# A two-layer hybrid decoder on one core: first projections from a transposed x, its root applied afterwards

## The chip, the cores and the metric

The kernel runs on one core of a Trainium2 chip. The metric is device time in microseconds, from timed runs of the whole program. Beside these there is one profiled execution, from which all views come. The engines are called PE (TensorE, with its weight loads as PEld), DVE (VectorE), ACT (ScalarE), POOL (GpSimd) and SP (SyncE, which issues nearly all DMAs).

## The reference

Two layers, x of 512 tokens by 1024 channels, all in float32. Per layer:

```
h = RMSNorm_pre(x)                       # x * rsqrt(mean(x*x) + 1e-6) * g_pre, per token
q_h, f_h, i_h, z_h, q_a, k_a, v_a, z_a = split(h @ W_in)
o_h = hgrn2(q_h, f_h, i_h) -> per-head RMSNorm, * silu(z_h)
q_a, k_a = rotary(q_a), rotary(k_a)      # 16 query heads, 2 key/value heads of 64
o_a = sliding-window attention (128) with sinks, * silu(z_a)
x = x + RMSNorm_post(concat(o_h, o_a) @ W_out)
```

The root of a token, rsqrt(mean(x*x) + 1e-6), is one number per token. So h @ W equals (x * g_pre) @ W with each token's row multiplied by its root afterwards.

## The kernel before

**Arithmetic.** Every large product is done as three matmuls in a rounded float type: each operand is split into a high part (a cast on ACT) and a low part (value minus high part, on DVE or POOL), and high·high, high·low and low·high are added in PSUM. The activations stand transposed, as `hT[l] = (hhi, hlo)`, 128 channels per partition block (8 blocks k) by 512 tokens.

**Weights.** All weights are one long list of pieces of 128 by 512 (256 KB), planned at L115 to L140 in the order of use: four of keys/values (`("kv", 0)`), then eight per slab of 512 columns, first the two query slabs `QA` and `QA + 1`. `w_load` (L156) issues a piece's DMA on SP into one of four raw buffers; `w_conv` (L165) makes high part (L181, ACT) and low part (L182, DVE, or POOL for pieces in `on_pool` with an odd number) in one of nine buffers each. A piece's load waits until the piece four before it is converted.

**Order.** `pin` (L84) keeps an instruction in the order in which the program issues it on its engine; other instructions may be moved by the scheduler that arranges the program when it is built. A `Unit` (L217) is one output tile: eight steps k of three matmuls each. `step` (L276) does one unit step, and two units run alternately from the half of the first on. `later(n, key, fn)` (L202) runs a function n steps on. `plan_conversions` (L247) gives each piece a step by which its conversion is issued. `merge` (L50) mixes steps with attention and recurrence work.

**The head of layer 0.** x comes in rows, four tiles `xts` of 128 tokens (L990 to L1005), with the kv pieces between them on SP. Per tile a `Norm` (L368) does: squares with a sum on ACT (L383, L386), the root on POOL (L354 or L391 and L393), scaling by root and gain on DVE (L401), eight transposes on PE (L406), high part on ACT (L410), low part on DVE (L414). The gain is spread over the partitions by eight transposes into two PSUM tiles (L1020). L1024 to L1074 write the order out by hand: tile 0 first, then kv for tile 0, with the later tiles' `half` calls between the kv steps. `kv_evac` (L448) copies a kv tile out of PSUM and loads the rotary tables; `kv_rotate` (L460) and `kv_store` (L486) rotate and transpose the keys.

**Queries.** `qa_stream` (L501) runs the four units of a query slab, m = 0 to 3, one after another (two at a time overlapping). `evac` multiplies the result by the cosine and sine tables on DVE (L510 to L517); at odd m POOL combines them (L520, L521), and `rest` splits (L526, L527), writes a stack to DRAM (L529) and reads it back in another layout (`load_q`, L497). Attention begins `QWAIT` steps after the second stack (L977 to L980). `constants` (L1089) loads masks and small parameters and prepares them, 36 steps after the start.

Of the kernel before, what the change touches and what calls it, by code (L numbers as in the profile page):

```python
# [25 lines left out]
EPS = 1e-6  # L26
# [6 lines left out]

W_BUFS = 9
# [36 lines left out]
def hybrid_kernel(ctx: ExitStack, tc: tile.TileContext, x, wkv, win, wout, g_pre, g_post, lbp, ghead, sinks,  # L71
# [50 lines left out]
    def plan_in(l, s):  # L122
        plan(("in", l, s), [win[l, s, k * P:(k + 1) * P, :] for k in range(KT)])
# [23 lines left out]
    in_turn = set(range(KT // 2, KT))  # L147
# [6 lines left out]
    state = {"raw": 0, "conv": 0, "limit": KT // 2}  # L154
# [92 lines left out]
    def plan_conversions():  # L247
# [15 lines left out]
        for p in reversed(range(len(pieces))):  # L263
            late = min(late, first[p] - LEAD) if p not in kv_pieces else late
            due.insert(0, late)
            late -= SPACE
# [101 lines left out]
    class Norm:  # L368
# [12 lines left out]
        def square(self, c=None, whole=None):  # L381
            if c is None:
                return pin(nc.scalar.activation(self.hT[1][:, :, self.tt * P:(self.tt + 1) * P],  # L383
                                                whole.rearrange("p a (k t) -> p (a k) t", t=P), AF.Square,
                                                scale=1.0 / 32.0, accum_out=self.ss[:, 0:1]))
            return nc.scalar.activation(self.hT[1][self.part(c)], self.xt[c].rearrange("p (k t) -> p k t", t=P), AF.Square,  # L386
                                        scale=1.0 / 32.0, accum_out=self.ss[:, c:c + 1])

        def power(self):
            t = sm.tile([P, 1], F32, tag="s1", name="s1")  # L390
            pin(nc.gpsimd.tensor_scalar(t, self.ss[:, 0:1], EPS, None, op0=ALU.add))  # L391
            self.r = sm.tile([P, 1], F32, tag="r1", name="r1")
            pin(nc.gpsimd.tensor_tensor(self.r, t, mhalf[:, 0:1], op=ALU.pow))  # L393

        def square_halves(self):
            for c in range(2):
                pin(self.square(c))
            self.r = rstd2(self.ss, pin)
# [44 lines left out]
    def layer(l, last):  # L443
# [3 lines left out]

        def kv_evac(tt, o):  # L448
            if tt == 0:
                rkv.append(big.tile([P, NT, 256], F32, tag="oy", name="rkv", bufs=6))  # L450
                rot.append(big.tile([P, 2, 512], F32, tag="q", name="cs", bufs=QB))
                nc.sync.dma_start(rot[0][:, 0], cos_f)
                nc.sync.dma_start(rot[0][:, 1], sin_f)
            nc.scalar.copy(rkv[0][:, tt], o)
            if tt == NT - 1:
                later(12 if l == 0 else 8, None, kv_rotate)
                later(24 if l == 0 else 16, ("k", l, 0), kv_store)


        def kv_rotate():  # L460
# [8 lines left out]
            kk = rkv_rot()  # L469
# [505 lines left out]
        def run():  # L975
            rest = lambda key: (through(key), remaining(key))
            until(lambda: 1 in qs)  # L977
            for _ in range(QWAIT):
                step()
# [200 lines left out]
```

## Time and profile before

| | us |
|---|---|
| timed runs, median (lowest to highest) | 921.15 (920.98 to 921.52) |
| profiled execution, its own time | 922.98 |
| its span | 921.3 |
| busy: PE, PEld, DVE, ACT, POOL | 904.2, 752.5, 667.0, 463.8, 273.9 |
| first kv matmul, first query matmul start | 10.06, 26.92 |

In the views, a timeline row gives start, duration, engine, line, operation, output<-inputs, shape and count, and in brackets how long the engine had been idle and what ended that. A group row ends in busy time, mean ns of one, idle time before it. Durations of matmuls overlap, so their pace is read from the distance of the starts.

### The profile page before, as it was taken

To read this page: it belongs to the slowest core of one execution; us is meant where nothing else is said; L and a number is where in the kernel's file an instruction comes from. 1 tells how busy PE (TensorE), PEld (TensorE's weight loads), DVE (VectorE), ACT (ScalarE), POOL (GpSimd) and SP (SyncE) were. 2 spreads that over 40 slices of the span, in tenths; PEclk is the share of its full clock that TensorE was granted. 3 is DMA by queue.
4 is the path that set the end of the run, shared out by engine and by line. 5 is a ranking of instruction groups with operands and counts; after the bars stand their busy time and mean duration, and the time that the engine had idled before them with its cause. 6 is when DMAs were issued, how large, how long until landed. Compare 5 with 4: busy or idle time off the path is not lost.

```text
span 921.3 us, 19004 instructions
## 1 busy us (share of the span) xinstructions
PE 904.2 (98%) x7240; PEld 752.5 (82%) x7240; DVE 667.0 (72%) x1326; ACT 463.8 (50%) x1100; POOL 273.9 (30%) x292
## 2 busy tenths in 40 slices
PE   8999999999999999999999999999999999999996
PEld 6888887888888888888888878888888888888885
DVE  4977878859854797655786689776889449866556
ACT  5535757653664423534563466686446463245242
POOL 3424444303413042121332254451144022330102
PEclk9999999999999999999999999999999999999999
DMA  7594613322222332333355656122322323213413
GB/s 224 153 259 130 172 43 92 92 81 85 91 69 70 107 103 82 92 95 119 131 168 167 168 141 179 57 70 92 94 70 81 99 73 94 82 47 93 137 35 137
DMA packets 56570, 100.74 MB, mean 109 GB/s; under 512 B 6560, under 2 KB 9120, under 8 KB 56480
## 3 DMA queue, kind: packets, MB, share of 16 engines
q1 hardware_dynamic: 56192, 99.40, 36.4%
q8 instruction: 57, 0.93, 0.4%
q14 instruction: 33, 0.27, 0.1%
q10 hardware_dynamic: 288, 0.14, 0.1%
HBM read 86.93 MB, written 12.58 MB: 108 GB/s over the span
## 4 chain that ended last, share of the span: by engine, by line
PE 89%; DVE 6%; ACT 2%; issue 1%; POOL 1%; DMA 0%; POOLq 0%; DVEq 0%; ACTq 0%
PE pj L293 73%; PE sc L567 2%; PE ac L620 2%; PE sc L750 2%; PE ac L821 2%; DVE wlo L182 1%; PE ac L824 1%; PE ac L808 1%; PE sc L594 1%; ACT s L581 1%; PE sc L873 1%; PE sc L406 1%; PE sc L796 1%; DVE a L954 0%; PE sc L556 0%
## 5 line engine op out<-in xcount | busy, mean ns | idle before, releaser
L182 DVE TENSOR_TENSOR wlo<-raw,whi 128x512 fp32r<-128x512 f32 x249 | 182.8, 748 | 49.5 <-ACT whi L181 48.8
L181 ACT CAST whi<-raw 128x512 fp32r<-128x512 f32 x256 | 154.1, 620 | 105.9 <-PE pj L293 95.1
L293 PE MATMUL pj<-hhi,wlo 128*128 128x512 f32 x512 | 203.8, 398 | 0.0
L293 PE MATMUL pj<-hhi,whi 128*128 128x512 f32 x512 | 199.8, 390 | 0.0
L293 PE MATMUL pj<-hlo,whi 128*128 128x512 f32 x512 | 199.5, 390 | 0.0
L293 PE MATMUL pj<-whi,ops 128*128 128x512 f32 (+1 forms) x520 | 172.5, 394 | 0.0
L293 PEld LDWEIGHTS pj<-whi,ops 128*128 128x128 f32 x520 | 97.3, 188 | 19.3
L293 PEld LDWEIGHTS pj<-hhi,whi 128*128 128x128 f32 x512 | 96.1, 188 | 20.7
L293 PEld LDWEIGHTS pj<-hhi,wlo 128*128 128x128 f32 x512 | 96.2, 188 | 19.3
L293 PEld LDWEIGHTS pj<-hlo,whi 128*128 128x128 f32 x512 | 96.2, 188 | 18.6
L293 PE MATMUL pj<-whi,hlo 128*128 128x512 f32 x256 | 103.6, 405 | 0.0
L293 PE MATMUL pj<-wlo,ops 128*128 128x512 f32 (+1 forms) x260 | 100.8, 388 | 0.0
L293 PE MATMUL pj<-wlo,hhi 128*128 128x512 f32 x256 | 100.4, 392 | 0.3 <-DVE wlo L182 0.2
L293 PE MATMUL pj<-whi,hhi 128*128 128x512 f32 x256 | 100.3, 392 | 0.0
L769 POOL TENSOR_TENSOR k<-k,tot 128x256 f32<-128x256 f32 x80 | 64.6, 835 | 106.0 <-PE sc L750 56.5
L581 ACT ACTIVATE s<-sc,negm 128x128 f32<-128x128 f32 x128 | 45.5, 368 | 38.5 <-DVE negm L575 38.5
L768 DVE TENSOR_TENSOR q<-q,tot 128x256 f32<-128x256 f32 x80 | 48.3, 641 | 12.8 <-PE sc L756 7.0
L293 PEld LDWEIGHTS pj<-whi,hhi 128*128 128x128 f32 x256 | 48.1, 188 | 10.3
L293 PEld LDWEIGHTS pj<-wlo,ops 128*128 128x128 f32 x260 | 49.0, 188 | 8.8
L293 PEld LDWEIGHTS pj<-wlo,hhi 128*128 128x128 f32 x256 | 48.3, 189 | 8.8 <-DVE wlo L182 1.0
L293 PEld LDWEIGHTS pj<-whi,hlo 128*128 128x128 f32 x256 | 48.2, 188 | 8.1
L588 POOL TENSOR_TENSOR s<-s,sums 128x512 f32<-128x512 f32 x32 | 34.1, 1066 | 44.2 <-DVE sums L586 29.2
(188 smaller groups left out, 1418.1 us busy)
## 6 DMA issues: line engine op xcount, KB each, us to landing
raw<-in_win_dram SPq DMA_DIRECT2D x192, 256.0 KB, 2.7
raw<-in_wout_dram SPq DMA_DIRECT2D x64, 256.0 KB, 2.7
stack<-rot SPq DMA_DIRECT2D x16, 512.0 KB, 3.4
qs<-stack SPq DMA_DIRECT2D x32, 256.0 KB, 4.7
a<-in_x_dram SPq DMA_DIRECT2D x12, 256.0 KB, 3.7
raw<-in_wkv_dram SPq DMA_DIRECT2D x8, 256.0 KB, 4.1
x_mid<-a SPq DMA_DIRECT2D x8, 256.0 KB, 2.6
a<-x_mid SPq DMA_DIRECT2D x8, 256.0 KB, 3.2
```

The costliest lines, as they stand in the source:

```text
L181: keep(nc.scalar.copy(hi, v))
L182: keep((nc.gpsimd if i in on_pool and i % 2 else nc.vector).tensor_tensor(lo, v, hi.bitcast(F32), op=ALU.subtract))
L293: nc.tensor.matmul(u.o, lhsT=u.sta(k, u.w)[i], rhs=u.mov(k, u.w)[j], start=(n == 0), stop=(n == len(u.list) - 1))
L406: pin(nc.tensor.transpose(o[:, j * P:(j + 1) * P], self.xn[:, c, j * P:(j + 1) * P], ident))
L567: pin(nc.tensor.matmul(S[:, h * 256:(h + 1) * 256], lhsT=q[:, 2 * hp_ + h, t_], rhs=kst[v][p][:, (n - 1) * P:(n + 1) * P], start=(h == 0 a ...
L581: nc.scalar.activation(pt[:, h * P:(h + 1) * P], cur[h], AF.Exp, bias=negm[:, h:h + 1], scale=SCALE, accum_out=sums[:, h:h + 1])
L588: nc.gpsimd.tensor_tensor(pv, pv, sums.unsqueeze(2).broadcast_to([P, 4, P]), op=ALU.mult)
L620: pin(nc.tensor.matmul(U, lhsT=vst[v][:, blk, :], rhs=d, start=(i == 0), stop=(i == len(terms) - 1)))
L750: pin(nc.tensor.matmul(L[32 * b:32 * b + 32, c:c + 16], lhsT=k[:, o_:o_ + 32], rhs=qv[:, blk:blk + qu, 1, :], start=True, stop=True, tile_ ...
L768: nc.vector.tensor_tensor(qv[:, :, 1, :], qv[:, :, 1, :], tv[:, :, 0].unsqueeze(2).broadcast_to([P, nb, hh]), op=ALU.mult)
L769: nc.gpsimd.tensor_tensor(kv_[:, :, 0, :], kv_[:, :, 0, :], tv[:, :, 1].unsqueeze(2).broadcast_to([P, nb, hh]), op=ALU.mult)
L821: pin(nc.tensor.matmul(O[:, c], lhsT=A[:, c], rhs=vs(j, n), start=(n == 0), stop=False))
```

## The change

A second input `xt` holds x transposed (1024 by 512). The head is replaced by `first_slabs`, called where the first query slab was enqueued:

- SP loads the eight tiles of `xt` with the four kv pieces between them; the x rows come after the loads of the first four query pieces.
- Per block k, ACT makes `hhi` = xt times gain (rounded), DVE `hlo` = xt times gain minus `hhi`. There are no transposes of x and no root in it. kv runs over k with all four token tiles open at once in the two `ac` PSUM tiles, 12 matmuls per k.
- Then ACT takes the squares of the four x tiles, POOL makes all four roots (`rcol`), PE spreads them over the partitions by four transposes into a PSUM tile `R`. `kv_evac` multiplies by the root while copying.
- The first query slab runs with its four units together, one column k at a time (`column`), in four PSUM tiles; its pieces are planned in the order `FIRST`. Its results are multiplied by rotary tables that contain the root (`rotr`).
- Behind its last use, each block k of `hhi` and `hlo` is rewritten with the root: multiply by gain and `R` on DVE into PSUM, high part on ACT, low part on DVE (`norm_high`, `norm_low`). Blocks 6 and 7 are rewritten after the slab's last matmul.
- Pieces 4 to 14 are converted in written order; the first slab's first four never on POOL, odd pieces of the second slab from its third on are. Key rotation, key transposes and constants are put 6, 10 and 10 steps into the second slab; attention begins two steps later after the second stack.

```diff
+FIRST = (0, 2, 4, 6, 1, 3, 5, 7)
...
+        order = FIRST if (l, s) == (0, QA) else range(KT)
+        plan(("in", l, s), [win[l, s, k * P:(k + 1) * P, :] for k in order])
...
+    on_pool.difference_update(slab_first["in", 0, QA][0] + j for j in range(4))
+    on_pool.update(slab_first["in", 0, QA + 1][0] + j for j in range(2, KT))
+    in_turn = set(range(KT // 2, KT // 2 + KT + 3))
...
+            if l == 0:
+                nc.scalar.activation(rkv[0][:, tt], o, AF.Copy, scale=rcol[:, tt:tt + 1])
+                return
...
-                if g < 2:
+                if g < 2 and not wait:
                     rest()
                 else:
-                    later(ROT_WAIT, None, rest)
+                    later(wait or ROT_WAIT, None, rest)
...
+    load_xt(0)
+    w_load(1)
+    for j in range(1, KT // 2):
+        load_xt(2 * j - 1)
+        load_xt(2 * j)
+        w_load(j + 1)
+    load_xt(KT - 1)
...
+        warm = sc_tiles[2]
+        for n in (512, 512, 256):
+            pin(nc.tensor.matmul(warm[:, 0:n], lhsT=ones[:, 0:P], rhs=ones[:, 0:n], start=True, stop=True))
...
+        def high(k):
+            pin(nc.scalar.activation(hhi[:, k, :], xk(k), AF.Copy, scale=gcol[:, k:k + 1]))
+
+        def low(k):
+            pin(nc.vector.scalar_tensor_tensor(hlo[:, k, :], xk(k), gcol[:, k:k + 1], hhi[:, k, :].bitcast(F32),
+                                               op0=ALU.mult, op1=ALU.subtract))
...
+        for j in range(KT // 2):
+            high(2 * j)
+            whigh(j)
+            low(2 * j)
+            high(2 * j + 1)
+            wlow(j)
+            low(2 * j + 1)
+            kv(2 * j)
+            kv(2 * j + 1)
+            w_load(KT // 2 + j + 1)
+        for tt in range(NT):
+            nc.sync.dma_start(xts[tt], x[tt * P:(tt + 1) * P, :].rearrange("p (a c) -> p a c", a=2))
+        base = state["conv"] = KT // 2
+        w_conv(base + 4)
+        w_load(base + KT)
...
+        for tt in range(NT):
+            pin(nc.scalar.activation(xts[tt], xts[tt], AF.Square, scale=1.0 / 32.0, accum_out=ss[:, tt:tt + 1]))
...
+        pin(nc.gpsimd.tensor_tensor(rcol, t, mhalf, op=ALU.pow))
...
+        def norm_high(k):
+            b = ac_tiles[k % 2]
+            pin(nc.vector.scalar_tensor_tensor(b, xk(k), gcol[:, k:k + 1], R, op0=ALU.mult, op1=ALU.mult))
+            pin(nc.scalar.copy(hhi[:, k, :], b))
+
+        def norm_low(k):
+            pin(nc.vector.tensor_tensor(hlo[:, k, :], ac_tiles[k % 2], hhi[:, k, :].bitcast(F32), op=ALU.subtract))
...
+        column(0)
+        column(1)
+        column(2, (0, 1))
+        w_conv(base + KT)
+        for tt in range(NT):
+            pin(nc.tensor.transpose(R[:, tt * P:(tt + 1) * P], rcol[:, tt:tt + 1].broadcast_to([P, P]), ident))
+        for tt in range(NT):
+            kv_evac(tt, o[tt // 2][:, tt % 2 * 256:tt % 2 * 256 + 256])
+        column(2, (2, 3))
+        norm_high(0)
+        norm_high(1)
+        norm_low(0)
+        load_tables()
+        norm_high(2)
+        norm_low(1)
+        column(3)
+        norm_high(3)
+        norm_low(2)
+        norm_low(3)
...
+        column(4)
+        norm_high(4)
+        norm_low(4)
+        w_conv(base + KT + 1)
+        for i in range(2):
+            pin(nc.vector.tensor_tensor(rotr[:, i], rot[0][:, i], R, op=ALU.mult))
+        column(5)
+        norm_high(5)
+        norm_low(5)
+        for m, wait in ((0, 0), (1, 3), (2, 0)):
+            qa(m, 6)
+            qa(m, 7)
+            qa_evac(m, acc[m], rotr, wait)
+        qa(3, 6)
+        qa(3, 7)
+        norm_high(6)
+        norm_high(7)
+        norm_low(6)
+        w_conv(base + KT + 2)
+        norm_low(7)
+        qa_evac(3, acc[3], rotr, 6)
+        emitted.update(("h", 0, tt) for tt in range(NT))
+        later(6, None, kv_rotate)
+        later(10, ("k", 0, 0), kv_store)
+        later(10, None, constants)
```

More of the change, by code (lines that the diff above doesn't have):

```diff
@@ L263, in plan_conversions @@
         for p in reversed(range(len(pieces))):
-            late = min(late, first[p] - LEAD) if p not in kv_pieces else late
+            late = min(late, first[p] - LEAD) if p in first and p not in kv_pieces else late
             due.insert(0, late)
@@ L379, in part, with square @@
             return (slice(None), slice(4 * c, 4 * c + 4), slice(self.tt * P, (self.tt + 1) * P))
[L381 to L385, printed above, removed]
+        def square(self, c):
             return nc.scalar.activation(self.hT[1][self.part(c)], self.xt[c].rearrange("p (k t) -> p k t", t=P), AF.Square,
                                         scale=1.0 / 32.0, accum_out=self.ss[:, c:c + 1])
[L389 to L398, printed above, removed]
         def scale(self, c):
@@ L446, in layer, with load_tables @@
         kst, vst, rot, oa, rkv = [], [], [], [], []
+        def load_tables():
+            rot.append(big.tile([P, 2, 512], F32, tag="q", name="cs", bufs=QB))
+            nc.sync.dma_start(rot[0][:, 0], cos_f)
+            nc.sync.dma_start(rot[0][:, 1], sin_f)
         def kv_evac(tt, o):
@@ L504, in qa_stream, with evac @@
             hold = {}
-            def evac(m, o):
-                cosf, sinf = rot[0][:, 0], rot[0][:, 1]
+            def evac(m, o, tables=None, wait=0):
+                t = tables or rot[0]
+                cosf, sinf = t[:, 0], t[:, 1]
                 if m % 2 == 0:
@@ L965, in layer @@
         for s_ in ORDER:
+            if s_ == "kv" and l == 0:
+                continue
             if s_ == "kv":
@@ L977, in run @@
             until(lambda: 1 in qs)
-            for _ in range(QWAIT):
+            for _ in range(QWAIT if l else QWAIT + 2):
                 step()
@@ L1014, in hybrid_kernel @@
     nc.vector.memset(ones, 1.0)
-    warm = pj()
-    gpre = [ac() for _ in range(2)]
-    pin(nc.tensor.matmul(warm, lhsT=ones[:, 0:P], rhs=ones, start=True, stop=True))
-    for k in range(KT):
-        pin(nc.tensor.transpose(gpre[k // 4][:, k % 4 * P:(k % 4 + 1) * P], gcol[:, k:k + 1].broadcast_to([P, P]), ident))
-    pin(nc.tensor.matmul(warm, lhsT=ones[:, 0:P], rhs=ones, start=True, stop=True))
-    hT[0] = new_hT()
-    head = [Norm(tt, [xts[tt][:, 0], xts[tt][:, 1]], gpre, hT[0]) for tt in range(NT)]
@@ L1025, in kv_high @@
-    def kv_high(i, eng):
-        raw = raws.pop(i)
-        conv[i] = tuple(big.tile([P, 512], F32R, tag="v", name="wkv", bufs=8) for _ in range(2))
-        pin(eng(conv[i][0], raw))
-        return lambda eng: pin(eng(conv[i][1], raw, conv[i][0].bitcast(F32), op=ALU.subtract))
-    A, V, G = nc.scalar.copy, nc.vector.tensor_tensor, nc.gpsimd.tensor_tensor
-    C = nc.vector.tensor_copy
-    m, n = head[0], head[1]
-    m.square_halves()
-    low0 = kv_high(0, A)
-    low1 = kv_high(1, A)
-    pin(m.scale(0))
@@ L1114, in constants @@
         pin(nc.vector.tensor_tensor(lb_c, lb, lb_b, op=ALU.subtract))
-    later(8 * NT + 4, None, constants)
     for run in [layer(l, l == DEPTH - 1) for l in range(DEPTH)]:
```

117 lines of the change are left out of this document (54 added, 63 removed).

## The prediction

> **What bounds the kernel now.** I read the page first, then busy time by stages, then TensorE's (PE's) own timeline over the first 60 us. From the page:
>
> ```profile
> span 921.3 us, 19004 instructions
> PE 904.2 (98%) x7240; PEld 752.5 (82%) x7240; DVE 667.0 (72%) x1326; ACT 463.8 (50%) x1100; POOL 273.9 (30%) x292
> PE 89%; DVE 6%; ACT 2%; issue 1%; POOL 1%; DMA 0%; POOLq 0%; DVEq 0%; ACTq 0%
> ```
>
> PE is busy nearly all the time and the chain that ended last runs through it. By stages (columns: us, busy time of each engine with its count, granted clock, DMA share, GB/s):
>
> ```profile
> 0.00:5.00 5.00, 2.19 (x3) 0.65 (x4) 0.55 (x2) 1.89 (x3) 0.68 (x6) 1.00 0.57 131
> 5.00:10.00 5.00, 5.00 (x18) 3.65 (x18) 1.57 (x3) 2.85 (x7) 3.01 (x3) 1.00 1.08 377
> 10.00:15.00 5.00, 3.57 (x27) 3.31 (x26) 4.04 (x8) 2.87 (x8) 2.56 (x4) 1.00 0.94 310
> 100.00:200.00 100.00, 98.79 (x544) 81.24 (x543) 77.71 (x167) 68.37 (x174) 36.22 (x33) 1.00 0.36 103
> 200.00:400.00 200.00, 200.00 (x2280) 165.57 (x2279) 146.91 (x281) 92.13 (x194) 53.81 (x66) 1.00 0.28 82
> 600.00:800.00 200.00, 199.97 (x2113) 164.95 (x2111) 148.87 (x288) 106.46 (x214) 57.77 (x65) 1.00 0.28 84
> 910.00:921.30 11.30, 3.68 (x28) 3.36 (x26) 6.01 (x12) 1.74 (x6) 2.34 (x3) 0.88 0.37 134
> ```
>
> Behind the head PE has next to no idle time until 910 us. So a microsecond taken from the head should reach the end whole, if nothing else becomes late. The head in PE's timeline (start, us, line, names, shape, count):
>
> ```profile
> 1.53 2.07 PE L1018 MATMUL pj<-u 128*128 128x512 f32 x2 [1.53 <-DVE u L1014]
> 4.89 1.94 PE L1020 MATMUL ac<-ident,gcol 128*128 128x128 f32 x8 [1.28 <-DMA gcol<-in_gcol_dram]
> 10.06 0.95 PE L293 MATMUL pj<-wkv,hhi 128*128 128x256 f32 x4
> 10.85 0.68 PE L293 MATMUL pj<-wkv,hlo 128*128 128x256 f32 x4
> 11.37 0.88 PE L293 MATMUL pj<-wkv,hhi 128*128 128x256 f32 x6
> 14.63 0.51 PE L293 MATMUL pj<-wkv,hhi 128*128 128x256 f32 x2 [1.43 <-POOL wkv L1029]
> 16.25 2.07 PE L293 MATMUL pj<-wkv,hhi 128*128 128x256 f32 x15 [0.24 <-ACT hhi L410]
> 18.16 0.60 PE L406 MATMUL sc<-ident,xn 128*128 128x128 f32 x4
> 26.92 0.40 PE L293 MATMUL pj<-hhi,wlo 128*128 128x512 f32 x1
> 43.04 0.39 PE L293 MATMUL pj<-hhi,whi 128*128 128x512 f32 x1
> 43.27 1.03 PE L490 MATMUL sc<-ident,b 128*128 128x128 f32 x8
> 44.06 0.48 PE L293 MATMUL pj<-hhi,wlo 128*128 128x512 f32 x1
> ```
>
> Keys/values are 96 matmuls of 256 columns. Fifteen take 18.16 - 16.25 = 1.91 us, 0.127 us each, so 12.2 us in all; yet the first query matmul starts only at 26.92. The other 14.7 us are the wait for x and its root, transposes, and pieces that are not yet converted. A query matmul (512 columns) takes 0.227 us: 72 start from 26.92 to 43.04, (43.04 - 26.92)/71. The first slab's 96 are 21.8 us of work. Without the key transposes of L490 (0.8 us, which both kernels do), PE has done kv and the first slab's worth at 26.9 + 21.8 = **48.7 us**. I ask when the changed kernel has done the same.
>
> **The change, part by part.** *Start.* The changed kernel can multiply as soon as the first tile of the transposed x, the gain column and the first kv piece have landed and ScalarE (ACT) has made one high part of each. From the DMA issues of the first microsecond and ACT's timeline:
>
> ```profile
> a<-in_x_dram SPq DMA_DIRECT2D x1, 256.0 KB, 3.8
> gcol<-in_gcol_dram ACTq DMA_DIRECT2D x1, 4.0 KB, 4.0
> 0.78 0.41 ACTq L996 DMA_DIRECT2D gcol<-in_gcol_dram  x1
> 4.60 0.63 ACT L386 ACTIVATE hlo<-a 128x512 fp32r<-128x512 f32 x1 [1.87 <-DMA a<-in_x_dram]
> 6.11 1.36 ACT L1028 CAST wkv<-raw 128x512 fp32r<-128x512 f32 x2
> ```
>
> The first x half is there at 4.6 us, the gain at 0.78 + 4.0 = 4.8. Then 0.63 (high part with the gain) and 0.68 (half of 1.36): kv starts at 4.85 + 0.63 + 0.68 = 6.2 us instead of 10.06, and no root or transposes stand before it. The eight gain transposes (L1020) and 32 transposes of x (L406) go.
>
> *Does kv then run dry?* Two k-steps need 768 KB and are 24 x 0.127 = 3.05 us of PE work. At the 377 GB/s of the second stage 768 KB are 2.1 us. ACT has three instructions for them (3 x 0.65 = 2.0 us) and VectorE (DVE) three (3 x 0.65). PE stays the slowest. But its first matmuls are slow: four took 10.85 - 10.06 = 0.79 us, 0.20 each, and from 10.85 on 0.13. PE had then worked without a break since 4.89, for 6.0 us. The changed kernel warms up from 1.53 on (two and a half times L1018's work). If the 6 us count from there, kv is slow until 7.5; if they count from 6.2, until 12.2. A slow microsecond loses 1 - 0.127/0.20 = 0.37. So 0.5 to 2.2 us; I take 0.5, since the old break was 1.3 us and the new one is some 0.4. [...] kv ends at 6.2 + 12.2 + 0.5 = **18.9 us**.
>
> *The root.* PE next runs ten of 32 (unit, k) steps, 30 matmuls or 6.8 us, until 25.7; then four transposes of the root, in fixed order. The root needs 2.1 MB of x in rows, behind 2.1 MB of transposed x, 1.05 of kv and 1.05 of query pieces. Its own steps in the trace:
>
> ```profile
> 16.57 1.07 ACT L383 ACTIVATE hlo<-x 128x1024 fp32r<-128x1024 f32 x1
> 17.53 0.20 ACT L383 ACTIVATION_READ_ACCUMULATOR hlo<-x 128x1 f32 x1
> 17.82 0.22 POOL L391 TENSOR_SCALAR s<-ss 128x1 f32<-128x1 f32 x1 [2.34 <-ACT hlo L383]
> 18.12 0.57 POOL L393 TENSOR_TENSOR r<-s,mhalf 128x1 f32<-128x1 f32 x1
> 14.97 1.04 PE L406 MATMUL sc<-ident,xn 128*128 128x128 f32 x8
> ```
>
> [...] Four PE transposes wait for it, and with them every query matmul queued behind on PE. They cost 4 x 0.13 = 0.5. The kv results' scaling on ACT also waits for the root, with the rewriting's first copies queued behind it; both have columns 2 and 3 (4 us) as cover. The first slab ends at 18.9 + 21.8 + 0.5 = 41.2 us. That is 48.7 - 41.2 = **7.5 us** ahead of before.
>
> *The rewriting.* This is what the change adds: per k a multiply into PSUM and a subtraction on DVE, a copy on ACT that waits until PE has read column k (behind it on ACT stand the high parts of pieces 12 and 13, wanted from 41 us on); also two multiplies for the rooted tables. All of it lies under columns 3 to 7 except the end. DVE's prices:
>
> ```profile
> 40.50 0.68 DVE L516 TENSOR_TENSOR rot<-pj,cs 128x512 f32<-128x512 f32 x1
> 41.10 0.68 DVE L517 TENSOR_TENSOR rot<-pj,cs 128x512 f32<-128x512 f32 x1
> 41.70 1.40 DVE L182 TENSOR_TENSOR wlo<-raw,whi 128x512 fp32r<-128x512 f32 x1
> 42.52 1.72 POOL L521 TENSOR_TENSOR rot<-rot 128x512 f32<-128x512 f32 x1
> ```
>
> So 0.6 us each back to back. The four units end at 37.1, 38.5, 39.8 and 41.2. DVE, which has just finished k = 5 at about 37.7, then does six evacuations, two multiplies for k = 6 and 7, the low part of k = 6, of piece 13, and of k = 7: eleven operations, to 44.3. The next slab starts at 41.2 and wants piece 13 after 12 matmuls, at 43.9: roughly on time. One unit step later it wants piece 14, at 45.3; that low part stands behind k = 7 and perhaps behind the last evacuation (1.2): 44.9 to 46.1, so up to 0.8 late. Beside POOL, DVE's L182 took 1.40 instead of 0.68, and two or three POOL operations fall into this stretch (two per second unit, and odd pieces): 0.7 to 2.1 more. No row shows this queue itself; its bounds are 0 and 4.9 us (PE idle from 41.2 until DVE's queue is empty at 46.1), and I take **2.0**, from the two terms just named (0.8 and half of 0.7 to 2.1, rounded). [...]
>
> *Moved work.* Key rotation, key transposes, constants and both stack writes with their loads now all fall behind 41 us instead of beginning at 27, and SP's queue carries them among the weight loads. Pieces 12 to 15 give PE 16 steps of 0.68 us, 10.9 us, to cover it; I price this at nothing, with up to 2 us if the cover fails. Attention begins about five steps further into the second slab than before, some 4% denser: nothing, up to 1.
>
> **Sum**: 7.5 - 2.0 = 5.5 us. The profiled execution took 922.98 us (span 921.3 and 1.7 around it), so 917.5 there; the median of the timed runs is 921.15, 1.8 lower, so **915.6 us**, 0.6% faster.
>
> **The rivals.** [...]
>
> [...]
>
> *PE stays slow through half of kv* (the 6 us count from 6.2): 1.7 more, 917.3.
>
> *No change: the lead is given back later.* If the moved work keeps DVE or SP behind so that attention's first steps make PE wait, or attention's own waits grow. PE's waits over the whole span have as largest:
>
> ```profile
> PE sc L567 <- ACT s L581: 2.7, 5, 0.8
> PE pj L293 <- POOL wkv L1029: 1.4, 1, 1.4
> L527 DVE TENSOR_TENSOR rot<-rot 128x512 fp32r<-128x512 f32 x4 | 4.0, 1004 | 1.4 <-ACT rot L526 1.2
> L1097 DVE CAST masks<-u 128x512 uint8<-128x512 f32 x1 | 1.5, 1514 | 0.0
> ```
>
> The stack's subtractions (4.0) and the mask conversion (1.5) are 5.5 us, just the gain; if PE stood through them all the time would be 921.1. Against: today they cost PE nothing.
>
> **How the numbers follow.** A measurement of this kernel can tell about 0.2% (1.8 us) from no change. Forecast (own range 913.1, no slip and the clock up at once, to 918.5, slip 4.9) 0.60; mild root 0.14; slow clock 0.08; given back 0.09; slower by the root 0.09. The first three are faster: 0.82; same 0.09; slower 0.09. The range goes from 912.9 (slip zero, clock up at once) through the mild cases to 920.4, which leaves out slower and half of given back.
>
> **What would show it.** Right: L293's successor for kv starts near 6.2 and ends near 19; no PE gap at the root's transposes; first matmul of the second slab near 41; PE gaps of about 2 us between 43 and 50, released by DVE's low parts; the rest of the span as before, shifted. Wrong: a PE gap before the transposes, kv released by DMA, 256-column matmuls at 0.20 us past 9 us, or idle PE between 50 and 100 us above today's.

## The result and the profile after

The changed kernel takes 932.88 us (median of 4 runs, 932.7 to 933.96) against 921.07 (920.97 to 921.52) for the kernel before, run beside it. The ratio is 1.0129 [1.0117, 1.0142]: 11.8 us slower. I had forecast 915.6, so the sign was wrong.

The page of the changed kernel, its span, its engines and its last chain:

```profile
span 931.2 us, 18940 instructions
PE 903.0 (97%) x7206; PEld 748.9 (80%) x7206; DVE 674.3 (72%) x1334; ACT 469.3 (50%) x1106; POOL 270.5 (29%) x286
PE 81%; DVE 10%; issue 5%; ACT 3%; POOL 1%; POOLq 0%; DVEq 0%; ACTq 0%
```

The busy totals have hardly moved (PE 904.2 to 903.0, DVE 667.0 to 674.3). What has moved is the chain: PE carries 81% of it instead of 89%, DVE 10% instead of 6%, "issue" 5% instead of 1%. PE's timeline shows that the head did what it was meant to do:

```profile
5.59 0.82 PE L1048 MATMUL ac<-wkv,hhi 128*128 128x256 f32 x4
17.31 0.40 PE L1085 MATMUL pj<-hhi,whi 128*128 128x512 f32 x1
25.36 0.65 PE L1104 MATMUL sc<-ident,rcol 128*128 128x128 f32 x4 [1.06 <-POOL rcol L1076]
40.82 0.39 PE L297 MATMUL pj<-hhi,wlo 128*128 128x512 f32 x1
43.32 0.39 PE L297 MATMUL pj<-hhi,whi 128*128 128x512 f32 x1
46.48 0.77 PE L297 MATMUL pj<-hhi,wlo 128*128 128x512 f32 x1 [2.78 <-DVE wlo L186]
47.05 0.63 PE L297 MATMUL pj<-hlo,whi 128*128 128x512 f32 x1
47.48 0.63 PE L297 MATMUL pj<-hhi,whi 128*128 128x512 f32 x1
50.01 0.40 PE L297 MATMUL pj<-hhi,whi 128*128 128x512 f32 x1
60.18 1.97 PE L487 MATMUL sc<-ident,b 128*128 128x128 f32 x8 [2.29 <-ACT b L471]
92.33 0.63 PE L595 MATMUL sc<-ident,s 128*128 128x128 f32 x4 [2.37 <-ACT es L585]
```

Keys/values start at 5.59 instead of 10.06, the query slab at 17.31 instead of 26.92, and the second slab at 40.82; its equivalent before was 48.7. Up to there the change leads by 7.9 us. Then come three gaps: 2.78 us for a weight's low part, 2.29 for the keys, 2.37 in attention, and after the first of them the distance of matmuls is 0.43 us (47.48 - 47.05) instead of 0.227: the eight from 46.48 to 50.01 take 3.53 us instead of 1.82. The same in the busy time of stretches (us; PE, PEld, DVE, ACT, POOL, then the granted clock, DMA share, GB/s), the kernel after:

```profile
40.00:45.00 5.00, 3.70 (x17) 2.74 (x15) 4.32 (x8) 2.22 (x5) 2.54 (x2) 1.00 0.00 0
45.00:50.00 5.00, 3.52 (x8) 2.79 (x9) 5.00 (x7) 2.69 (x5) 4.09 (x3) 0.66 0.22 60
50.00:60.00 10.00, 7.88 (x35) 6.19 (x33) 10.00 (x16) 4.03 (x7) 3.85 (x3) 1.00 0.72 228
60.00:70.00 10.00, 9.82 (x41) 8.36 (x42) 9.42 (x27) 3.18 (x7) 2.54 (x2) 0.83 0.92 262
100.00:200.00 100.00, 94.01 (x466) 76.00 (x465) 79.72 (x182) 67.75 (x187) 43.58 (x39) 1.00 0.35 101
```

From 45 to 60 us DVE has not one idle moment, while PE has 3.6 (15.00 - 3.52 - 7.88). And far behind the head, from 100 to 200 us, PE is busy for 94.01 us where it was 98.79 before: attention, which the change doesn't touch, has waits that it didn't have.

**Where the time goes: two marks.** Layer 0's attention has a first score matmul and a last value matmul. The rows of both, with the steps that lead to the first score, first in the kernel before (DVE's first multiply of the first query units' results, the split of the finished rotation, the loading of the first query stack on SP, the first score, the last values):

```profile
38.02 0.68 DVE L510 TENSOR_TENSOR rot<-pj,cs 128x512 f32<-128x512 f32 x1
43.25 1.55 DVE L527 TENSOR_TENSOR rot<-rot 128x512 fp32r<-128x512 f32 x1
47.77 2.93 SPq L500 DMA_DIRECT2D qs<-stack  x4
61.16 1.00 PE L556 MATMUL sc<-kst,qs 128*128 128x128 f32 x8
172.25 0.62 PE L620 MATMUL ac<-pprev,vst 128*128 128x512 f32 x2
```

then in the changed kernel:

```profile
38.27 0.68 DVE L508 TENSOR_TENSOR rot<-pj,csr 128x512 f32<-128x512 f32 x1
50.97 4.68 DVE L525 TENSOR_TENSOR rot<-rot 128x512 fp32r<-128x512 f32 x4
57.95 5.23 SPq L497 DMA_DIRECT2D qs<-stack  x4
76.56 1.00 PE L557 MATMUL sc<-kst,qs 128*128 128x128 f32 x8
182.01 0.61 PE L621 MATMUL ac<-pprev,vst 128*128 128x512 f32 x2
```

These two fences hold most of the answer. The slab as a whole ends 8 us earlier, but attention wants only the first two of its four units, and those arrive at the same time as in this trace of before, 38.27 against 38.02 (and later than in e2 and e18, two runs with the head of before, where DVE's first multiply comes at 36.28 and 35.57): four units that run together all end late. From there every step falls further behind: the split by 7.7 us (DVE's queue holds rewriting and low parts ahead of it), the stack's loading by 10.2, the first score by 15.4. The last value is 9.8 us late and so is the end: the spans differ by 931.2 - 921.3 = 9.9. The other 1.9 of the 11.8 lie in the profiled execution of before, which ran 1.8 us above its median (more on that below).

**A check of this reading over all runs.** The table has, from each run's trace, the start of the second slab, how many of its projection matmuls and those of the next slab stand ahead of the first score in PE's order, the starts of first score and last value, the time between them, and the time from the last value to the start of PE's last instruction. The ratio is to the kernel before, run beside it; its median lay between 920.98 and 921.89 in the groups of runs, so a difference of less than 1 us between rows of different groups is not shown by their times.

| run | second slab | matmuls ahead | first score | last value | between | from there to the end | time, us | ratio to before |
|---|---|---|---|---|---|---|---|---|
| before | 49.6 | 51 | 61.2 | 172.5 | 111.3 | 740.9 | 921.07 | |
| after | 40.8 | 115 | 76.6 | 182.2 | 105.7 | 741.2 | 932.88 | 1.0129 [1.0117, 1.0142] |
| e1 | 41.5 | 118 | 77.2 | 185.4 | 108.2 | 742.0 | 935.97 | 1.015 [1.0133, 1.0167] |
| e2 | 47.9 | 90 | 68.3 | 177.8 | 109.5 | 740.7 | 928.17 | 1.0068 [1.0053, 1.0083] |
| e3 | 40.8 | 111 | 72.3 | 178.6 | 106.3 | 741.5 | 930.84 | 1.0095 [1.008, 1.011] |
| e4 | 41.9 | 119 | 74.0 | 181.4 | 107.3 | 740.9 | 933.64 | 1.0123 [1.0108, 1.0138] |
| e5 | 41.1 | 60 | 63.1 | 185.2 | 122.1 | 740.9 | 933.47 | 1.0138 [1.0123, 1.0153] |
| e6 | 41.5 | 60 | 63.4 | 182.7 | 119.3 | 742.0 | 933.08 | 1.0127 [1.011, 1.0144] |
| e7 | 43.0 | 60 | 64.5 | 184.5 | 120.0 | 740.7 | 933.84 | 1.0136 [1.012, 1.0151] |
| e8 | 46.4 | 72 | 68.3 | 180.0 | 111.7 | 741.8 | 930.26 | 1.0102 [1.0087, 1.0117] |
| e9 | 41.0 | 106 | 73.1 | 180.6 | 107.4 | 741.0 | 931.55 | 1.0107 [1.0092, 1.0122] |
| e10 | 40.4 | 72 | 63.3 | 173.8 | 110.6 | 741.3 | 926.49 | 1.0047 [1.0032, 1.0062] |
| e11 | 50.0 | 69 | 67.4 | 177.5 | 110.2 | 740.5 | 928.09 | 1.0068 [1.0053, 1.0083] |
| e12 | 41.1 | 60 | 61.8 | 181.0 | 119.2 | 741.1 | 931.96 | 1.0111 [1.0094, 1.0128] |
| e13 | 43.5 | 72 | 62.5 | 173.0 | 110.5 | 741.0 | 923.33 | 1.0018 [1.0009, 1.0028] |
| e14 | 44.0 | 72 | 65.1 | 175.6 | 110.5 | 740.9 | 925.91 | 1.0046 [1.0031, 1.0061] |
| e15 | 46.5 | 60 | 68.0 | 188.2 | 120.1 | 741.9 | 939.92 | 1.02 [1.0185, 1.0216] |
| e16 | 46.9 | 60 | 67.7 | 184.2 | 116.5 | 741.5 | 935.44 | 1.015 [1.0133, 1.0167] |
| e17 | 41.0 | 115 | 76.5 | 181.5 | 104.9 | 740.5 | 932.31 | 1.0124 [1.0107, 1.014] |
| e18 | 47.2 | 51 | 58.7 | 167.0 | 108.3 | 740.6 | 917.53 | 0.9966 [0.9953, 0.9979] |

In twenty traces the last column of times is 741.2 give or take 0.8. So everything that the change does to the end is decided at the last value of layer 0's attention, some 180 us in. The kernel's order says why: `merge` spreads the projections up to slab `FQ` over attention, and in the traces of both kernels the same 561 projection matmuls stand ahead of the last value. A later first score moves some of them from behind it to ahead of it and takes none away; what moves the last value is PE's waits, its pace and the work of the head. The first column of times decides nothing: e5 and e13 begin the second slab at 41.1 and 43.5 and end 10 us apart. What sets the last value was not clear at first; the experiments are told in the order in which the theories fell.

### The profile page after: what moved, and what is told of

Read it like the earlier page. It is cut to its first block, busy times and chain, and to the rows that moved or that the text cites. A ratio compares the mean times of both kernels' runs of the same rounds, so it can differ in the third digit from the quotient of the medians.

```text
span 931.2 us, 18940 instructions
## 1 busy us (share of the span) xinstructions
PE 903.0 (97%) x7206; PEld 748.9 (80%) x7206; DVE 674.3 (72%) x1334; ACT 469.3 (50%) x1106; POOL 270.5 (29%) x286
## 4 chain that ended last, share of the span: by engine, by line
PE 81%; DVE 10%; issue 5%; ACT 3%; POOL 1%; POOLq 0%; DVEq 0%; ACTq 0%
PE pj L297 67%; PE sc L751 2%; PE sc L568 2%; PE ac L621 2%; DVE wlo L186 2%; PE ac L822 2%; ACT s L582 1%; PE ac L825 1%; PE ac L809 1%; DVE rot L525 1%; PE sc L595 1%; PE sc L874 1%; DVE mx L573 1%; DVE ac L1089 1%; DVE a L955 1%
## 5 line engine op out<-in xcount | busy, mean ns | idle before, releaser
L186 DVE TENSOR_TENSOR wlo<-raw,whi 128x512 fp32r<-128x512 f32 x248 | 184.2, 758 | 59.2 <-ACT whi L185 58.3
L297 PE MATMUL pj<-hhi,wlo 128*128 128x512 f32 x480 | 192.6, 401 | 2.8 <-DVE wlo L186 2.8
L297 PE MATMUL pj<-hhi,whi 128*128 128x512 f32 x480 | 188.0, 392 | 0.0
L297 PE MATMUL pj<-hlo,whi 128*128 128x512 f32 x480 | 187.8, 391 | 0.0
L297 PE MATMUL pj<-whi,ops 128*128 128x512 f32 (+1 forms) x520 | 172.5, 394 | 0.0
L297 PEld LDWEIGHTS pj<-hhi,wlo 128*128 128x128 f32 x480 | 90.8, 189 | 21.3 <-DVE wlo L186 3.2
L297 PEld LDWEIGHTS pj<-hhi,whi 128*128 128x128 f32 x480 | 90.7, 189 | 19.6
L297 PEld LDWEIGHTS pj<-hlo,whi 128*128 128x128 f32 x480 | 91.0, 190 | 17.4
L582 ACT ACTIVATE s<-sc,negm 128x128 f32<-128x128 f32 x128 | 45.7, 370 | 40.8 <-DVE negm L576 40.7
```

Of the source, the lines that this page charges most:

```text
L186: keep((nc.gpsimd if i in on_pool and i % 2 else nc.vector).tensor_tensor(lo, v, hi.bitcast(F32), op=ALU.subtract))
L297: nc.tensor.matmul(u.o, lhsT=u.sta(k, u.w)[i], rhs=u.mov(k, u.w)[j], start=(n == 0), stop=(n == len(u.list) - 1))
L582: nc.scalar.activation(pt[:, h * P:(h + 1) * P], cur[h], AF.Exp, bias=negm[:, h:h + 1], scale=SCALE, accum_out=sums[:, h:h + 1])
```

## The experiments

**First theory: the stall at piece 13.** The largest single gap (2.78 us) and the slow matmuls after it stand where the prediction had its slip. *e1* moves that low part ahead of the last evacuations:

```
         norm_low(5)
+        w_conv(base + KT + 2)
         for m, wait in ((0, 0), (1, 3), (2, 0)):
...
         norm_low(6)
-        w_conv(base + KT + 2)
         norm_low(7)
```

> The changed kernel with the conversion of piece 13 issued ahead of the units' last steps instead of between the rewriting of blocks 6 and 7. Stall theory (the time is lost where PE waits between 41 and 64 us): the wait of 2.8 us for that low part and the slow clock behind it (8 matmuls at 0.43 instead of 0.23 us, 1.6 us) go, and 4 us of it reach the end: 928.9 against 932.9. Late-attention theory (the time is lost between 80 and 160 us, because attention's inputs come late and its work then stands too dense): attention's inputs come no earlier, PE only waits for them longer; 1.5 us or less, 931.5 to 933.

It took 935.97, three us *more* than the changed kernel, above both ranges. Its largest waits of PE (total, times, longest):

```profile
PE sc L487 <- ACT b L471: 4.1, 1, 4.1
PE sc L595 <- ACT es L585: 3.3, 1, 3.3
...
PE pj L297 <- DVE wlo L186: 0.6, 1, 0.6
```

The stall is gone (0.6), and the keys' wait has grown from 2.3 to 4.1, attention's from 2.4 to 3.3. The theory falls: the gap was one place where a late queue shows, not the cause. Two more of the same kind, *e3*, which keeps the second slab's low parts off POOL,

```
-    on_pool.update(slab_first["in", 0, QA + 1][0] + j for j in range(2, KT))
+    on_pool.difference_update(slab_first["in", 0, QA + 1][0] + j for j in range(KT))
```

> The changed kernel with no low part of the second query slab on POOL. If DVE and POOL holding each other up is what makes DVE late from 47 to 56 us (six DVE operations of 0.6 us take 8.2 us there): the key rotation and the stacks come about 3 us earlier and the time falls by 2 to 4 us, 929 to 931. If not, DVE has two or three more operations and the time is the same or 1 us longer, 933 to 934.

and *e4*, which rotates the first keys on POOL and early:

```
+            eng = nc.vector if l else nc.gpsimd
...
+        kv_rotate()
         column(2, (2, 3))
...
+        later(2, ("k", 0, 0), kv_store)
...
-        later(6, None, kv_rotate)
-        later(10, ("k", 0, 0), kv_store)
```

> The changed kernel with the first layer's key rotation moved to POOL and issued right behind the root (POOL is idle from 30 to 40 us), and the key transposes two steps into the second slab. Stall theory: the wait of 2.3 us before the key transposes and the slow clock behind it (1.2 us) go, and DVE loses 4 us of work where it is late: 928 to 930. Late-attention theory: attention still waits for the query stacks, so 1 to 2 us at most, 931 to 932.

e3 took 930.84 (2.0 less, in its first range), e4 933.64 (no gain, outside both). In e4 the keys are transposed at 46.2 instead of 60.2 us, and the first score still comes only at 74.0: keys alone were not what it waited for.

**Second theory: attention merely begins too late in PE's order** (behind 115 projection matmuls instead of 51). *e2* does that alone to the kernel before:

```
-            for _ in range(QWAIT):
+            for _ in range(QWAIT if l else QWAIT + 19):
```

> The kernel before, with attention of the first layer begun 19 unit steps later and nothing else: its first scores then stand about as far into the projections as in the changed kernel. Late-attention theory: this alone makes the kernel before slower by 5 to 9 us, 926 to 930. Stall theory: attention has room, less than 1 us, 921 to 922.

It took 928.17, 6.5 us more, with nothing else changed. The first score stands behind 39 more matmuls (39 x 0.227 = 8.9 us) and the stretch to the last value shrinks by only 1.8, though PE has 8.9 us less to do in it. So a later first score costs by itself. PE's largest waits in attention show how, in the kernel before, in e2, and (three lines) in the changed kernel:

```profile
PE sc L567 <- ACT s L581: 1.0, 2, 0.8
```

```profile
PE sc L567 <- ACT s L581: 6.5, 6, 1.5
```

```profile
PE sc L568 <- ACT s L582: 3.3, 4, 1.3
PE sc L595 <- ACT es L585: 2.4, 1, 2.4
PE sc L595 <- POOL s L589: 1.9, 2, 1.2
```

Projections that were issued ahead of the first score are missing as filler behind it, and PE waits for attention's own softmax on ACT and POOL. But *e5*, which splits and loads the changed kernel's first query stack at once,

```
-        for m, wait in ((0, 0), (1, 3), (2, 0)):
+        for m, wait in ((0, 0), (1, 0), (2, 0)):
```

> The changed kernel with one number changed: the first query group's split and its write to DRAM are issued with the evacuation of unit 1 instead of three steps into the second slab. In the order of the built program the first attention scores then stand behind 60 projection matmuls of the second slab on PE, against 115 in the changed kernel and 51 in the kernel before. Late-attention theory: a delay of 39 matmuls cost the kernel before 6.5 us, so taking away 55 gives 6 to 9 us: 924 to 927. Stall theory: the waits before 64 us stay or grow by one more DVE operation: 932 to 934.

has the first score at 63.1 instead of 76.6 us, and took 933.47, in the range of the stall theory. Order alone falls too: waits for the second slab's low parts now stand first, as PE's waits of e5 show.

```profile
PE pj L297 <- DVE wlo L186: 5.3, 2, 4.9
PE pj L297 <- POOL wlo L186: 4.2, 1, 4.2
```

**Third theory: DVE has no room.** Low parts, keys, query stacks, masks and constants are all DVE's work, and the change puts 18 operations of some 0.6 us behind the root (two per block of x and two for the tables). Over the whole span DVE has only 8 more, 1334 against 1326, since the head needs fewer; what counts is the stage. Busy time of the two stretches, the kernel before and then the changed one:

```profile
26.00:45.00 19.00, 19.00 (x94) 15.99 (x93) 18.32 (x38) 9.80 (x20) 8.91 (x6) 1.00 0.60 178
45.00:70.00 25.00, 25.00 (x120) 20.94 (x119) 17.96 (x33) 8.55 (x23) 6.91 (x5) 1.00 0.89 247
```

```profile
26.00:45.00 19.00, 17.70 (x79) 14.31 (x77) 16.55 (x25) 9.23 (x20) 5.44 (x4) 1.00 0.36 112
45.00:70.00 25.00, 21.23 (x83) 17.35 (x84) 24.42 (x48) 9.89 (x18) 10.48 (x7) 0.86 0.70 208
```

Before, DVE was already busy for 18.32 of 19 us under the first slab, and free for 7 of the next 25; after, it is busy for 24.42 of these 25. *e11* puts 16 multiplies whose result nobody reads into the kernel before, four ahead of each evacuation of its first slab:

```
+                if (l, s) == (0, 0):
+                    for _ in range(4):
+                        pin(nc.vector.tensor_tensor(extra, o, cosf, op=ALU.mult))
```

> The kernel before with 16 more multiplies of 128 by 512 on DVE, four ahead of each evacuation of the first query slab, into a tile that nothing reads. Full-DVE theory: the kernel before has no room either (DVE busy 15.7 of 16.3 us from 26.9 to 43.2), 10 us of work put off the stacks and attention; 3 to 7 us slower, 924 to 928. If DVE has slack: under 1 us.

It took 928.09, as the full-DVE theory had it: 16 operations of DVE cost 6.2 us though PE's work is the same. *e9* takes the rewriting (all `norm_high` and `norm_low`) out of the changed kernel, *e10* does that with e5's first stack:

```
-        norm_high(0)
-        norm_high(1)
-        norm_low(0)
...
-        norm_low(7)
```

> The changed kernel without rewriting the eight blocks (16 operations on DVE and 8 on ACT left out, so that everything behind the first slab uses x without its root). Full-DVE theory (DVE is busy throughout from 30 to 70 us, and whatever stands last in its queue makes PE wait: attention's inputs, the key transposes or a weight's low part): DVE has 10 us less to do, 6 to 10 us less time, 923 to 927. If order alone is at fault (attention late by its place in the program, 106 matmuls in): 2 us at most, 931 to 933.

> The last kernel with the first stack written at once as well (first scores 72 matmuls in). Full-DVE theory: with room on DVE the earlier attention does help, unlike in the run with the rewriting: PE keeps its lead of 8 us but for a few, 914 to 919. If the earlier stack is no help in itself: as the last run, 923 to 927.

e9 took 931.55, 1.3 less than the changed kernel (2.0 by the ratios), in the range of order alone; e10 926.49, 7.0 less than e5 and 5.1 less than e9, so that the earlier stack does help there, but far above the 914 to 919 of the full-DVE theory. So the rewriting is dear in one order and cheap in another: load and order act together. Four attempts keep the whole computation and relieve DVE's queue. *e6* is e5 with e3's line; *e7* adds e4's edits to e6; *e8* adds piece 13 as in e1 and `constants()` ahead of `column(0)`; *e12* is e6 with x loaded between the query pieces and its squares between their high parts, so that the root comes earlier (after the first two columns).

> The last kernel with no low part of the second slab on POOL as well. If the two causes add: 2 us less than with the early stack alone, 922 to 925. If the earlier stack already takes away what POOL cost: the same within 0.5 us.

> The last kernel with the key rotation on POOL behind the root and the key transposes at step 2 as well. With attention early, the stalls before 64 us should count now: stall theory as a second cause gives 2 to 4 us more, 918 to 922. If DVE's own queue is what is late, 1 us at most.

> The last kernel with piece 13 converted ahead of the units' last steps and the constants issued before the first query column, where DVE is idle. The wait of 2.8 us for piece 13 and its slow clock should go and PE keep most of its lead of 8 us: 915 to 919, below the kernel before. Against it stands that the first scores come 12 matmuls later in the program's order (72): then 919 to 922.

> The changed kernel with the x rows loaded between the first query pieces instead of behind them, the root spread after two columns (about 22.5 us instead of 25.4), the first stack at once and no low part of the second slab on POOL. Full-DVE theory: DVE starts on the rewriting 3 us sooner, in time that it idles now, and all that follows is 3 us sooner: 929 to 930.5 against 933.1 with the late root. If DVE is not the bound there: 932.5 to 934.

They took 933.08, 933.84, 930.26 and 931.96: e6 and e7 as their second readings had it, e8 far above both of its ranges, e12 between its two. Each relieves the wait that it is aimed at and another takes its place: low parts 7.5 us in e6, the keys' transposes 4.1 in e7, an evacuation 3.7 in e8, low parts 7.0 in e12.

**The load alone, in doses.** *e13*, *e14* and *e15* share one arrangement (keys rotated right behind their eviction and transposed at step 2, constants ahead of the columns, first stack at once) and have none, the first four blocks, or all of the rewriting:

```
+        constants()
         column(0)
...
+        kv_rotate()
...
+        later(2, ("k", 0, 0), kv_store)
+        for m, wait in ((0, 0), (1, 0), (2, 0)):
```

> Another arrangement: the first keys are rotated on DVE right behind their eviction and transposed two steps into the first slab's tail, the masks and constants come before the first columns of the root, the first query stack is transposed at once; and all 16 rewriting operations on x and its halves are left out, so x is never put on its root and the output is not the reference's. Full-DVE theory: without the 16 operations (10 to 11 us of DVE's time) the support work gets done before PE's next needs, and PE's lead of 8 us at the first slab's end reaches the end at least in good part: 914 to 920 us. Rival, order alone: the rewriting hardly matters in any arrangement, and this gives the same within 2 us as the same arrangement with the full rewriting.

> The same arrangement with the rewriting of the first four blocks of x only (8 of the 16 operations; the other blocks are left without their root and the output is not the reference's). Full-DVE theory: in between the none and the full version, about half way: 920 to 926 us. Order alone: the same as both.

> The same arrangement with all 16 rewriting operations, so the whole computation. Full-DVE theory: 926 to 933 us, that is 8 us or more above the version without rewriting, with DVE busy 97% or more of the stretch from 30 to 70 us. Order alone: whatever the arrangement gives, the same within 2 us as without the rewriting.

They took 923.33, 925.91 and 939.92. The first evacuation of a query unit on DVE and the busy time from 31 to 62 us, for none,

```profile
39.58 0.69 DVE L508 TENSOR_TENSOR rot<-pj,csr 128x512 f32<-128x512 f32 x1 [1.67 <-PE pj L1085]
31.00:62.00 31.00, 27.93 (x126) 22.64 (x125) 23.93 (x36) 9.68 (x17) 11.66 (x9) 1.00 0.56 170
```

half,

```profile
42.55 0.68 DVE L508 TENSOR_TENSOR rot<-pj,csr 128x512 f32<-128x512 f32 x1
31.00:62.00 31.00, 26.93 (x113) 21.59 (x114) 27.07 (x42) 12.04 (x21) 8.82 (x7) 0.94 0.57 170
```

and all:

```profile
45.05 0.68 DVE L508 TENSOR_TENSOR rot<-pj,csr 128x512 f32<-128x512 f32 x1
31.00:62.00 31.00, 23.86 (x88) 18.50 (x89) 28.44 (x47) 11.26 (x20) 7.79 (x6) 0.83 0.49 151
46.48 0.77 PE L297 MATMUL pj<-hhi,wlo 128*128 128x512 f32 x1 [3.95 <-DVE rot L509]
```

Without rewriting DVE waits for PE (1.67 us) before the first evacuation; with half it no longer does and is 3.0 late, with all 5.5, and PE then stands 3.95 us for a PSUM tile that DVE has not emptied. The "order alone" of these expectations falls: 16 operations, some 10 us of DVE, are worth 16.6 us here. It is no straight line: the first eight operations cost 2.6, the last eight 14.0. Of the last 14.0, 3.0 lie ahead of the first score and 9.6 in the stretch behind it (120.1 against 110.5), where PE waits 3.5 us for one low part on POOL; there the arrangement isn't quite the same either, 60 matmuls stand ahead of the first score in e15 and 72 in the other two. I had expected the half version halfway, the full one below 933, and DVE over 97% busy in it from 30 to 70 us. It was busy for 33.30 of these 40, 83%: the slowest run of all does not have a full DVE, but one that comes too late with the operation PE needs next. And my theory missed on the main point as well: *without* the rewriting I expected 914 to 920, and got 923.33. So the rewriting on DVE explains 16.6 us of this arrangement's time, and not why the new head doesn't win without it. *e16* puts together what had helped (e12's order, keys on POOL, constants early):

> The whole computation with what took load off DVE or out of its queue's way put together: no high part of the weights rounded on POOL, x loaded between the query pieces so that the squares come earlier, the first keys on POOL, the constants before the columns, the first query stack at once. Full-DVE theory: DVE keeps the 16 rewriting operations and the tables, so it stays at or above the kernel before, 923 to 930 us. Rival, order alone: with every step in its place the lead comes through, 913 to 918 us.

It took 935.44; both expectations missed. No version of the whole computation that I tried gets below e8's 930.26, and none with the new head beats the kernel before.

**Last theory: attention's chain sets the stretch, and PE's lead is lead in its filler.** e2 had hinted at it: less PE work between first score and last value hardly shortened the stretch. *e17* (changed kernel) and *e18* (kernel before) leave out one product of three in the third slab, under attention, and nothing of DVE's:

```
+            if n % 3 == 1 and u.key == ("in", 0, IV) and slab_done[u.key] < 48:
+                continue
```

> The changed kernel with 48 projection matmuls left out of PE's filler inside layer 0's attention: in the first 48 steps of the third projection slab the product with the activations' low half is skipped (the output is a little off), all else and DVE's work stay. 48 x 0.227 = 10.9 us less for PE between the first score and the last attention value. Chain theory (layer 0's attention takes 105 to 111 us from its first score on its own chain, and the end comes 741 us after its last value, as in every run so far): the interval is at its floor of 105.7 already, so the time falls by less than 4 us, to 929 or more. Rival, PE's work sets the stretch: it falls by 8 to 10.9 us, to 922 to 925.

> The kernel before with the same 48 matmuls left out. Chain theory: its interval of 111.3 us falls to the floor of about 105.5, so the time falls by 5 to 6 us, to 915 to 917. Rival, PE's work sets the stretch: it falls by 10.9 us, to about 910.5.

The expectations count wrongly: that slab has 32 steps, not 48, and the product left out is the weights' low part times the high part of x. The groups show it 256 times in the kernel before,

```profile
L293 PE MATMUL pj<-wlo,hhi 128*128 128x512 f32 x256 | 100.4, 392 | 0.3 <-DVE wlo L182 0.2
```

and 224 times in e18,

```profile
L295 PE MATMUL pj<-wlo,hhi 128*128 128x512 f32 x224 | 87.7, 391 | 0.2 <-DVE wlo L182 0.2
```

so 32 matmuls are gone, 32 x 0.227 = 7.3 us. e17 took 932.31, 0.6 less than the changed kernel; e18 917.53, 3.45 less than the kernel before beside it. From first score to last value, each in its kernel (before, e18, after, e17):

```profile
61.16:172.87 111.71, 110.39 (x568) 91.45 (x567) 92.37 (x206) 72.79 (x226) 53.99 (x48) 1.00 0.42 114
```

```profile
58.72:167.36 108.64, 104.50 (x536) 84.91 (x535) 93.25 (x206) 72.62 (x226) 53.41 (x48) 1.00 0.41 117
```

```profile
76.56:182.62 106.06, 97.05 (x504) 78.25 (x503) 85.91 (x199) 71.62 (x225) 52.11 (x45) 1.00 0.38 107
```

```profile
76.52:181.84 105.32, 92.50 (x472) 74.79 (x471) 83.77 (x198) 70.65 (x225) 52.52 (x45) 0.95 0.36 104
```

In the changed kernel 7.3 us less of PE's work shorten the stretch by 0.7. This isn't a clean test: the granted clock is 0.95 in e17 where it was 1.00, which I estimate at some 5 us of PE's time (0.05 x 105.32), so that PE's busy time falls by 4.6 only, and its idle time grows from 9.0 (106.06 - 97.05) to 12.8. The idle times alone say that PE's work doesn't set this stretch; what it would be with 7.3 us less at full clock is not shown. In the kernel before, at a clock of 1.00 in both, they shorten it by 3.1, less than half: there PE is busy for 110.39 of 111.71 us and still only partly the bound. PE's work as the sole bound falls for both. Where e18 lands (108.6) I had expected 105 to 106, and its time of 917.53 is a little above the 915 to 917 of the chain theory; so the floor isn't the same in both, and this size stays open, as does whether the stretch goes by DVE's share (92.37 of 111.71 us) or by the length of each scores-softmax-values chain. Nor did I try two units at a time with the new head.

**What the runs settle.** The two traces can be balanced at the last value, 172.47 us in the kernel before and 182.24 in the changed one. PE is idle up to there for 5.8 us before and 16.7 after:

| PE idle, us | up to the second slab | from there to the first score | from there to the last value |
|---|---|---|---|
| before | 4.5 | 0.0 | 1.3 |
| after | 2.6 | 5.1 | 9.0 |

The granted clock from 40.82 to 76.56 us is 0.90 instead of 1.00, by my estimate some 3.6 us more (0.10 x 35.74). Idle 10.9 more, clock 3.6, and 9.8 in all leave -4.7 for the work of the head that is gone. So the change takes 6.6 us off the head in these traces (1.9 idle and 4.7 work) and pays 5.1 of waits ahead of the first score, 7.7 behind it and 3.6 of slow clock. The waits behind it are those that e2 makes in the kernel before by a later first score alone; those ahead of it go to what DVE does late, the low part and the keys, and e11 and e13 to e15 show that work put into DVE's queue there lengthens the time. How much of the whole is due to each alone isn't separated, since every version that took one wait away got another.

Layer 0's attention takes 105 to 112 us from its first score in most versions, and 116 to 122 in e5, e6, e7, e12, e15 and e16, where only 60 matmuls stand ahead of it in the new head and PE waits in it for low parts (1.2 to 4.6 us); 741 us follow. The kernel before starts it at 61.2, or 58.7 in e18. No version with the new head starts it before 61.8 (e12). Its first two query units are done no earlier (38.27 against 38.02), and their road to the first score leads through DVE's queue; yet in e10 and e13, without the rewriting, the first score comes only at 63.3 and 62.5, behind 72 matmuls, so DVE is not all of it. The 8 us that PE leads at the second slab are a lead on projections, which are filler beside attention's chain.

## Why the prediction was wrong, step by step

- *kv at 6.2, over at 18.9.* It was 5.59 and 17.31: better than forecast. The clock was no loss here: it was granted at 1.00 in each 5 us up to 20 us.
- *No wait for the root.* The sum has the four transposes run at 25.7 without one. That x would be in early enough for this was my estimate, and no run shows it: in the changed kernel the loads of x were issued from 13.53 to 15.38 and took 5.7 us (the first two, median) and 7.3 (the last two) to land, the squares ran from 18.84 to 23.84, POOL had the root at 25.31, and the transposes waited 1.06 us, to 25.36. So the gap that I had named as a sign of being wrong was there. The first slab ended on time all the same.
- *First slab over at 41.2, 7.5 ahead.* Right: 40.82. But the 48.7 beside it came from one execution whose start was late. e18 leaves the start untouched, and its first kv matmul there is

```profile
8.07 0.73 PE L295 MATMUL pj<-wkv,hhi 128*128 128x256 f32 x4
```

  2.0 us before the 10.06 of the quoted trace, in which PE had waited 1.28 us for the gain column; in e2 and e11, with the same head, it is at 8.64 and 8.61. The head that the change replaces was therefore worth some 1.5 to 2 us less than I took it for, and I subtracted the 1.8 between execution and median from a kernel that no longer has that start.
- *A slip of 2.0 at piece 13.* PE did wait for a low part of DVE's (2.78 us), but the forecast had 13 "roughly on time" and 14 late (by its own rows wanted one unit step of 0.68 after 43.9, so at 44.6 and not 45.3). Piece 13 itself was late: DVE did it from 45.74 to 46.42 at the usual 0.68, behind two operations of block 5 that should have been over (37.61 and 39.47), one evacuation more than counted (45.15) and 0.68 us in which DVE waited for ACT's copy. The size was short by the slow matmuls behind the wait, 3.53 - 1.82 = 1.7 more. It was also the wrong thing to count: e1 took it away and lost.
- *"I price this at nothing, with up to 2 us if the cover fails"* (the moved work), and *"about five steps further ... nothing, up to 1"* (attention). This is the step that failed. I covered the moved work with PE's 10.9 us of projections and never asked when DVE would do it. Attention's first score went from behind 51 matmuls to behind 115, so 21 steps further, not five: 64 x 0.227 = 14.5 us, plus 8.6 of waits and slow matmuls (76.56 - 40.82 = 35.7, less 115 x 0.227 = 26.1 and the key transposes), plus 1.0 of key transposes at full pace, minus the 8.8 by which the slab began earlier in the two traces (49.6 to 40.8) is 15.3, and 15.4 were measured. The stretch behind it gave 5.6 back, where 14.5 us of matmuls had left it: the rest went into PE's waits on attention's own steps, 9.0 us idle instead of 1.3. The idle time between 50 and 100 us that I had named as a sign of being wrong is there too.
- *"So a microsecond taken from the head should reach the end whole, if nothing else becomes late."* The premise was read from PE's 98%. A busy PE showed only that filler was there to fill it. Here its share is no measure of the bound, by e18's 3.1 of 7.3 us: a stretch in which PE is busy for 98.8% (110.39 of 111.71) shrank by less than half of what was taken away.
- *The rivals.* "Given back later" had the right mechanism, that moved work keeps DVE or SP behind, but its price was made of DVE's own 5.5 us, so that it ended at no change. It had no term for the first score's place in PE's order, and nothing in the forecast had one for the slow clock behind two of the waits (0.66 from 45 to 50 us, 0.83 from 60 to 70). The one slower case with a chance of its own was a late root; PE's wait for it was 1.06.

## What to carry to other kernels

Before a lead on the busiest engine is carried to the end, find the chain that the next stage starts with and ask whether *its* first input comes earlier; here the first two query units did not, and all else was filler. A move of work off the head must be charged to the queue that does it over the whole stretch: DVE stood at 18.32 of 19 us, and 16 operations more cost 6.2 us even in the kernel before. An engine that is busy for 99% of a stretch can be tested for being its bound by taking a few of its instructions away, if the clock is compared as well.

## What the runs showed of the hardware

- After PE had stood still for 2.78 us, its next eight matmuls took 1.7 us longer, at a distance of up to 0.57 us (46.48 to 47.05) and then 0.43, with a granted clock of 0.66 from 45 to 50 us; after 2.29 us, eight transposes took 1.97 instead of 1.03 (at 43.27 in the kernel before), at a clock of 0.83 from 60 to 70. So that wait of 2.8 us cost 4.5. After the 2.37 us before 92.33 the clock stayed at 1.00 from 92 to 95 us. In e17 it was 0.87 from 90 to 120 us, where the changed kernel had 1.00.
- In the changed kernel DVE's four subtractions of L525 at 50.97 took 4.68 us (1.17 each), with this on POOL at the same time:

```profile
51.75 3.35 POOL L186 TENSOR_TENSOR wlo<-raw,whi 128x512 fp32r<-128x512 f32 x2 [1.25 <-ACT whi L185]
```

  In e5 two of the same subtractions took 1.28 us at 53.37 (0.6 each), where POOL had nothing from 52.90 to 63.60. In the changed kernel three DVE operations from 45.74 to 47.54 took 0.6 each too, with POOL's L518 at work from 45.91 to 47.57. POOL's two took 1.7 each, against 1.29 for the same operation at 487.31, where DVE worked for 0.13 us of it. e3, without low parts of the second slab on POOL, was 2.0 us faster than the changed kernel; the same step from e5 to e6 gained 0.4.
- The start of the kernel before is uneven: the first kv matmul came at 10.06 us in one execution and at 8.07, 8.61 and 8.64 in e18, e11 and e2 with the same head.
